# A hybrid decoder layer on one core: a filler 64 bytes smaller, and another order in which a group's PSUM banks are emptied

## The chip, the cores and the metric

The kernel runs on one core of a Trainium2 chip. The metric is the device time of one execution in microseconds. The kernel before took 1816.91 us, the median of three runs (1816.64 to 1817.56 us).

## What is computed

One layer over 272 tokens (16 meta tokens and 256 others) of width 4096: a norm, one input projection to 16384 columns, sixteen heads of stick-breaking attention beside sixteen groups of a short convolution, and an output projection.

```python
h = rmsnorm(x, norm_g)
p = h @ w_in                      # 4096 -> q, k, v, g_attn, b, c, h, z: 8 x 2048
o = stick_breaking_attention(heads(q), heads(k), heads(v))
o = group_rmsnorm(o * silu(g_attn), attn_norm_g, 16)
y = b_conv * short_conv(c_conv * h_conv, conv_w)
y = group_rmsnorm(y * silu(z_conv), conv_norm_g, 16)
return x + concatenate([o, y]) @ w_out
...
return rmsnorm(hs, final_norm_g)[:, N_META:]
```

Everything is float32. The two projections are nearly all of the work.

## The kernel before

**The split.** TensorE multiplies in fp32r. Each weight piece of 128x1024 floats comes by DMA into a ring of five (`raw`). ScalarE casts it to its high part (`wh`, line 408), VectorE subtracts that to get the low part (`wl`, line 404), and each product is three matmuls: low by high, high by high, high by low. Rings of six hold `wh` and `wl`, and the casts run about five pieces ahead of TensorE.

**Pieces.** The program is one list of pieces, and instructions stand in each engine's queue in the order in which the code issues them. The first projection has eight groups `g`, each of two heads with their two convolution groups. Pieces of kind `p` are blocks of k, v, c and h: four pieces per block with the weights stationary and the tokens `xs` moving, 24 matmuls each, summed in a bank called `mm` (lines 441 to 443). Pieces `A`, `B`, `T`, `U` make the four remaining outputs with tokens stationary and weights moving, 512 columns wide (lines 449, 451, 452). For 14 of the 16 pairs of row blocks in a group from 1 on they use seven products in place of eight, for which sums of tokens (`sum`, `lent`) and of weights (`tt`) are made on the way.

**Eight PSUM banks.** Such a group has eight sums, one to a bank: four that are output quarters (D11, D12, D21, D22, the numbers 0 to 3) and four that are products to be shared among the quarters (P1, P5, P7, P6, the numbers 4 to 7). Sum q of group g lies in bank (q + 4g) mod 8, so that the next group's D sums use the banks of this group's P sums, and the other way round. A group has a first zone, in which only its D banks fill, and a second, in which all eight do. D22 is copied out between the two (`open_rows`) and its bank serves the blocks of the second zone.

**The end of a group.** After the last `U` piece of a group, the two last pieces of a block in D22's bank follow. In that time `evict` (lines 650 to 671) empties the seven other banks: ScalarE copies P1, and VectorE adds the products to the quarters, with the results in the tiles `cq` and `cb` (two rows of 512 floats each). What follows on TensorE is the last block of the group (head 1, kind h). Its bank is the one that held D11 (`block_bank`), so its first matmul waits until VectorE has read D11. Transposes of q for the attention (`qT`) and the next group's first pieces come behind that block's first half. Group 0 has no products, and its evict is four ScalarE copies.

**Order.** Nothing is sorted by costs: `later` gives small tasks (softmax, norm, transposes) a piece behind which they are issued, and `evict` is issued one piece after the group's last `U`. The second projection has four groups of the same kind and a thin rest of 256 columns (`mo`, lines 945 to 947); two of its eight weight pieces lie in tiles called `keep`, the others in the rings.

**Memory.** The pools are laid out one behind the other: constants, the small buffers `wk`, the rings `wp`, then the token sums and later the mixed rows `mixh` and `mixl`. The tokens `xs`, and after them the tail's tiles (`res`, `keep`, `osum`), are laid out from the other end. Fillers with the names `pad_...` hold nothing and only move what lies behind them. In the built program `wh0` starts at byte 61120 of a partition, `mixh0` at 114368, `xs0` at 147264 and the first `keep` at 212864.

Of the kernel before, what the change touches and what calls it, by code (L numbers as in the profile page):

```python
# [8 lines left out]
F32 = mybir.dt.float32  # L9
# [3 lines left out]
ALU = mybir.AluOpType  # L13
AX = mybir.AxisListType

P = 128
# [102 lines left out]
def kernel(ctx, tc, xt, xin, xm, par, fg, w1, w2, out):  # L119
# [3 lines left out]
    wk = ctx.enter_context(tc.tile_pool(name="wk", bufs=1))  # L123
    wp = ctx.enter_context(tc.tile_pool(name="wp", bufs=4))

    wp.tile([P, 56], F32, name="pad_w", bufs=1)
    wk.tile([P, 32], F32, name="pad_wk")
    pp = ctx.enter_context(tc.tile_pool(name="pp", bufs=1, space=bass.MemoryType.PSUM))
    dp = ctx.enter_context(tc.tile_pool(name="dp", bufs=1, space=bass.MemoryType.DRAM))

# [303 lines left out]
    psum = {}  # L434
# [22 lines left out]
    D11, D12, D21, D22, P1, P5, P7, P6 = range(8)  # L457
# [85 lines left out]
    V, A, G, T = nc.vector, nc.scalar, nc.gpsimd, nc.tensor  # L543
# [106 lines left out]
    def evict(g):  # L650
        s = gr[g]
        cq = s["cq"] = wk.tile([P, 2, 512], F32, tag="cq", name=f"cq{g}")
        cb = s["cb"]
        if g:
            p1, p5, p7, p6 = (psum.pop((g, q)) for q in (P1, P5, P7, P6))
            A.copy(out=cq[:, 0], in_=p1)
            V.tensor_tensor(out=cb[:, 0], in0=p6, in1=cq[:, 0], op=ALU.add)
            V.tensor_tensor(out=cq[:, 1], in0=p7, in1=cb[:, 0], op=ALU.add)
            V.tensor_tensor(out=cb[:, 1], in0=p5, in1=cb[:, 1], op=ALU.add)
            V.tensor_tensor(out=cb[:, 0], in0=p5, in1=cb[:, 0], op=ALU.subtract)  # L660
            V.tensor_tensor(out=cb[:, 1], in0=cb[:, 1], in1=cq[:, 1], op=ALU.subtract)
        for q, d in ((D11, cq[:, 0]), (D21, cq[:, 1]), (D12, cb[:, 0])):
            if g:
                V.tensor_tensor(out=d, in0=psum.pop((g, q)), in1=d, op=ALU.add)  # L664
            else:
                A.copy(out=d, in_=psum.pop((g, q)))
        if not g:
            A.copy(out=cb[:, 1], in_=psum.pop((g, D22)))
        for c, q in (("cq", "h"), ("cb", "c")):
            v = s[c].rearrange("p t (u w x) -> p t u w x", u=2, w=2)  # L670
            s[q] = v[:, :, :, 0, :], v[:, :, :, 1, :]
# [349 lines left out]
    for i in range(1 - SPLITS, n):  # L1021
# [28 lines left out]
        if i < n1:  # L1050
# [4 lines left out]
            if i in top.values():  # L1055
                later(i + 1, evict, p[1])
                if p[1] == GROUPS - 1:
                    open_mix(0)
            if i == n1 - 1:
                open_tail()  # L1060
        elif p[0] in "ABTUmk":
            g = p[1]
# [96 lines left out]
```

## Time and profile before

The profile is of one execution. Its chain of waits, its groups by line and its timeline are used below.

| | |
|---|---|
| median of three runs | 1816.91 us |
| the profiled execution's own time | 1819.97 us |
| its span, first to last instruction | 1818.2 us |
| VectorE busy | 1561.5 us (86%) |
| ScalarE busy | 1211.2 us (67%) |
| DMA, mean | 221 GB/s |
| first and last matmul | 1.1 us; 1806.6 us |
| granted TensorE clock | 0.998 |

A row of the groups reads: line, engine, operation, the tile written and those read, shape and count; then the busy time in us and the mean of one in ns; then the idle time just before them on that engine and what ended it. In the timeline, a row gives start and length in us, and in brackets the idle time of the engine before it. Matmuls overlap: one of 0.28 us is followed by the next after about 0.12 us, so lengths of matmuls don't add up, and starts do.

### The profile page before, as it was taken

Reading aid. Unit: us, or ns where it says so; the run is one execution under the profiler, and the core shown is the slowest. Engines: PE = TensorE matmul, PEld = TensorE weight load, DVE = VectorE, ACT = ScalarE, POOL = GpSimd, SP = SyncE. Lnnn points to the kernel's source line nnn. Section 1 sums busy time; section 2 is a strip of 40 time slices with the busy share of each in tenths; the row PEclk is TensorE's granted clock in tenths of the full one; section 3 lists DMA queues with packets and bytes.
Section 4 is the critical chain, followed back from the end, with each engine's and each line's share of the span. In section 5 each row is a group of like instructions: output and inputs, shape, how many; then the busy total and the mean of one; then the engine's idle time right before and its main releaser. Section 6 shows DMA issues by size and latency. Waiting matters only on the chain.

```text
span 1818.2 us, 29724 instructions
## 1 busy us (share of the span) xinstructions
PE 1794.0 (99%) x10968; PEld 1622.2 (89%) x10968; DVE 1561.5 (86%) x1936; ACT 1211.2 (67%) x2018; POOL 132.6 (7%) x176
## 2 busy tenths in 40 slices
PE   9999999999999999999999999999999999999997
PEld 7899999899989998899889988999899988888897
DVE  6775889888988898889888988898889898989895
ACT  6755776777667766776677667766776776555563
POOL 2131001010101010101010101010001010000000
PEclk9999999999999999999999999999999999999999
DMA  8877466756675667566756675667566677676665
GB/s 311 311 247 247 160 221 215 249 174 224 216 243 175 229 213 242 177 230 212 241 179 225 215 242 179 225 217 240 178 226 219 227 228 251 208 250 203 197 219 193
DMA packets 118515, 402.57 MB, mean 221 GB/s; under 512 B 13280, under 2 KB 18528, under 8 KB 118368
## 3 DMA queue, kind: packets, MB, share of 16 engines
q1 hardware_dynamic: 114336, 396.99, 65.7%
q10 hardware_dynamic: 4032, 3.67, 0.6%
q8 instruction: 86, 1.41, 0.3%
q14 instruction: 61, 0.50, 0.1%
HBM read 388.03 MB, written 12.58 MB: 220 GB/s over the span
## 4 chain that ended last, share of the span: by engine, by line
PE 88%; DVE 4%; ACT 4%; issue 2%; DMA 2%; ACTq 0%; DVEq 0%; SPq 0%
PE P L449 16%; PE P L451 16%; PE P L452 16%; PE mm L441 12%; PE mm L443 12%; PE mm L442 12%; ACT wh L408 2%; DVE wl L404 2%; DMA raw<-w 1%; ACT vv L577 1%; PE mo L947 0%; PE mo L945 0%; PE mo L946 0%; PE po L812 0%; PE z L756 0%
## 5 line engine op out<-in xcount | busy, mean ns | idle before, releaser
L404 DVE TENSOR_TENSOR wl<-raw,wh 128x1024 fp32r<-128x1024 f32 (+3 forms) x766 | 864.4, 1151 | 157.4 <-ACT wh L408 145.2
L408 ACT CAST wh<-raw 128x1024 fp32r<-128x1024 f32 (+3 forms) x766 | 723.1, 973 | 318.3 <-PE mm L442 88.4
L441 PE MATMUL mm<-xs,wh 128*128 128x258 f32 (+1 forms) x2048 | 589.9, 288 | 8.8 <-DVE cq L664 7.8
L442 PE MATMUL mm<-xs,wh 128*128 128x258 f32 (+1 forms) x2048 | 585.8, 286 | 0.0
L443 PE MATMUL mm<-xs,wl 128*128 128x258 f32 (+1 forms) x2048 | 585.5, 286 | 0.0
L441 PEld LDWEIGHTS mm<-xs,wh 128*128 128x128 f32 x2048 | 385.4, 188 | 15.9 <-ACT wh L408 10.1
L442 PEld LDWEIGHTS mm<-xs,wh 128*128 128x128 f32 x2048 | 385.4, 188 | 3.9
L443 PEld LDWEIGHTS mm<-xs,wl 128*128 128x128 f32 x2048 | 387.1, 189 | 0.0
L408 ACT CAST wh<-t 128x1024 fp32r<-128x1024 f32 (+1 forms) x118 | 123.2, 1044 | 171.3 <-DVE t L425 123.9
L449 PE MATMUL P<-wh,xs 128*128 128x512 f32 x534 | 211.5, 396 | 1.6 <-ACT wh L408 1.6
L451 PE MATMUL P<-wh,xs 128*128 128x512 f32 x534 | 210.4, 394 | 0.0
L452 PE MATMUL P<-wl,xs 128*128 128x512 f32 x534 | 209.1, 392 | 0.0
L449 PE MATMUL P<-wh,mixl 128*128 128x512 f32 (+1 forms) x412 | 155.8, 378 | 0.0
L452 PE MATMUL P<-wl,mixh 128*128 128x512 f32 (+1 forms) x412 | 155.0, 376 | 0.0
L451 PE MATMUL P<-wh,mixh 128*128 128x512 f32 (+1 forms) x412 | 155.0, 376 | 0.0
L404 DVE TENSOR_TENSOR wl<-t,wh 128x1024 fp32r<-128x1024 f32 (+1 forms) x118 | 144.1, 1221 | 6.2 <-ACT wh L408 6.2
L425 DVE TENSOR_TENSOR t<-raw,raw 128x1024 f32<-128x1024 f32 (+1 forms) x118 | 144.0, 1220 | 0.0
L452 PEld LDWEIGHTS P<-wl,xs 128*128 128x128 f32 x534 | 100.6, 188 | 23.1
L449 PEld LDWEIGHTS P<-wh,xs 128*128 128x128 f32 x534 | 100.7, 189 | 19.9 <-ACT wh L408 1.9
L451 PEld LDWEIGHTS P<-wh,xs 128*128 128x128 f32 x534 | 100.9, 189 | 16.8
L449 PE MATMUL P<-wh,lent 128*128 128x512 f32 x252 | 101.1, 401 | 0.0
L451 PE MATMUL P<-wh,lent 128*128 128x512 f32 x252 | 98.7, 392 | 0.0
(247 smaller groups left out, 2086.0 us busy)
## 6 DMA issues: line engine op xcount, KB each, us to landing
raw<-w SPq DMA_DIRECT2D x614, 512.0 KB, 4.4
lent<-sumd SPq DMA_DIRECT2D x63, 512.0 KB, 6.1
raw<-w SPq DMA_DIRECT2D x32, 384.0 KB, 3.8
sumd<-lent SPq DMA_DIRECT2D x9, 512.0 KB, 5.8
raw<-xin SPq DMA_DIRECT2D x8, 512.0 KB, 5.7
raw<-mixd SPq DMA_DIRECT2D x8, 512.0 KB, 4.7
xr<-xt SPq DMA_DIRECT2D x15, 272.0 KB, 5.1
res<-xin SPq DMA_DIRECT2D x12, 256.0 KB, 4.7
```

Of the source, the lines that this page charges most:

```text
L404: nc.vector.tensor_tensor(out=lo[:, c], in0=t[:, c], in1=h[:, c].bitcast(F32), op=ALU.subtract)
L408: nc.scalar.copy(out=h[:, c], in_=t[:, c])
L425: nc.vector.tensor_tensor(out=s[:, :2 * hw].rearrange("p (a b) -> p a b", a=2), in0=a[:, :2 * hw].rearrange("p (a b) -> p a b", a=2), in1= ...
L441: nc.tensor.matmul(out=o, lhsT=h, rhs=x[:, 0, s:], start=k == 0, stop=False)
L442: nc.tensor.matmul(out=o, lhsT=h, rhs=x[:, 1, s:], start=False, stop=False)
L443: nc.tensor.matmul(out=o, lhsT=lo, rhs=x[:, 0, s:], start=False, stop=k == KC - 1)
L449: nc.tensor.matmul(out=o, lhsT=a[1], rhs=h, start=key not in begun, stop=False)
L451: nc.tensor.matmul(out=o, lhsT=a[0], rhs=h, start=False, stop=False)
L452: nc.tensor.matmul(out=o, lhsT=a[0], rhs=lo, start=False, stop=last)
L577: e(out=d[32 * j:32 * j + 32, :, 32 * i:32 * i + 32], in_=s[32 * i:32 * i + 32, :, 32 * j:32 * j + 32])
```

## The change

Two edits.

1. The filler `pad_wk` has 16 floats per partition instead of 32. All tiles of `wk` behind it, the rings, the token sums and the mixed rows start 64 bytes earlier: `wh0` at 61056, `mixh0` at 114304. Tokens, `res`, `keep` and `osum` stay where they are. `wh0` started 64 bytes past a multiple of 128 and now starts at one.
2. In `evict`, for groups 1 to 7, the addition that reads D11 stands second among the eight VectorE additions; it was sixth. The other seven keep their order. For group 0 the four copies stay as they are.

```diff
-    wk.tile([P, 32], F32, name="pad_wk")
+    wk.tile([P, 16], F32, name="pad_wk")
...
+        d11, d21, d12 = (psum.pop((g, q)) for q in (D11, D21, D12))
         if g:
             p1, p5, p7, p6 = (psum.pop((g, q)) for q in (P1, P5, P7, P6))
             A.copy(out=cq[:, 0], in_=p1)
-            V.tensor_tensor(out=cb[:, 0], in0=p6, in1=cq[:, 0], op=ALU.add)
-            V.tensor_tensor(out=cq[:, 1], in0=p7, in1=cb[:, 0], op=ALU.add)
-            V.tensor_tensor(out=cb[:, 1], in0=p5, in1=cb[:, 1], op=ALU.add)
-            V.tensor_tensor(out=cb[:, 0], in0=p5, in1=cb[:, 0], op=ALU.subtract)
-            V.tensor_tensor(out=cb[:, 1], in0=cb[:, 1], in1=cq[:, 1], op=ALU.subtract)
-        for q, d in ((D11, cq[:, 0]), (D21, cq[:, 1]), (D12, cb[:, 0])):
-            if g:
-                V.tensor_tensor(out=d, in0=psum.pop((g, q)), in1=d, op=ALU.add)
-            else:
-                A.copy(out=d, in_=psum.pop((g, q)))
-        if not g:
-            A.copy(out=cb[:, 1], in_=psum.pop((g, D22)))
+            for o, x, y, op in ((cb[:, 0], p6, cq[:, 0], ALU.add), (cq[:, 0], d11, cq[:, 0], ALU.add),
+                                (cq[:, 1], p7, cb[:, 0], ALU.add), (cb[:, 1], p5, cb[:, 1], ALU.add),
+                                (cb[:, 0], p5, cb[:, 0], ALU.subtract), (cb[:, 1], cb[:, 1], cq[:, 1], ALU.subtract),
+                                (cq[:, 1], d21, cq[:, 1], ALU.add), (cb[:, 0], d12, cb[:, 0], ALU.add)):
+                V.tensor_tensor(out=o, in0=x, in1=y, op=op)
+        else:
+            for x, o in ((d11, cq[:, 0]), (d21, cq[:, 1]), (d12, cb[:, 0]), (psum.pop((g, D22)), cb[:, 1])):
+                A.copy(out=o, in_=x)
```

VectorE's queue at the end of group 1, before. The names of the banks' contents are P, the number of the sum and the group, so `P0_1` is D11 and `P7_1` is P6 of group 1; what a row waits for stands behind it.

```order
L404 TENSOR_TENSOR wl163_3889<-raw163_3847,wh163_3888 128x1024 [waits DMAHW1_49,PE_49,Activation_49]
L657 TENSOR_TENSOR cb1_2269<-P7_1_2318,cq1_3921 128x512 [waits PE_49,Activation_49]
L658 TENSOR_TENSOR cq1_3921<-P6_1_2297,cb1_2269 128x512 [waits DVE_49]
L659 TENSOR_TENSOR cb1_2269<-P5_1_2293,cb1_2269 128x512
L660 TENSOR_TENSOR cb1_2269<-P5_1_2293,cb1_2269 128x512 [waits DVE_49]
L661 TENSOR_TENSOR cb1_2269<-cb1_2269,cq1_3921 128x512 [waits DVE_49]
L664 TENSOR_TENSOR cq1_3921<-P0_1_2080,cq1_3921 128x512
L664 TENSOR_TENSOR cq1_3921<-P2_1_2084,cq1_3921 128x512 [waits DVE_49]
L664 TENSOR_TENSOR cb1_2269<-P1_1_2088,cb1_2269 128x512
L404 TENSOR_TENSOR wl164_3919<-raw164_3859,wh164_3918 128x1024 [waits DMAHW2_49]
```

The same place of the changed kernel:

```order
L404 TENSOR_TENSOR wl163_3889<-raw163_3847,wh163_3888 128x1024 [waits DMAHW1_49,PE_49,Activation_49]
L662 TENSOR_TENSOR cb1_2269<-P7_1_2318,cq1_3921 128x512 [waits PE_49,Activation_49]
L662 TENSOR_TENSOR cq1_3921<-P0_1_2080,cq1_3921 128x512 [waits DVE_49]
L662 TENSOR_TENSOR cq1_3921<-P6_1_2297,cb1_2269 128x512
L662 TENSOR_TENSOR cb1_2269<-P5_1_2293,cb1_2269 128x512
L662 TENSOR_TENSOR cb1_2269<-P5_1_2293,cb1_2269 128x512 [waits DVE_49]
L662 TENSOR_TENSOR cb1_2269<-cb1_2269,cq1_3921 128x512 [waits DVE_49]
L662 TENSOR_TENSOR cq1_3921<-P2_1_2084,cq1_3921 128x512 [waits DVE_49]
L662 TENSOR_TENSOR cb1_2269<-P1_1_2088,cb1_2269 128x512
L404 TENSOR_TENSOR wl164_3919<-raw164_3859,wh164_3918 128x1024 [waits DMAHW2_49]
```

Only the row that reads `P0_1` has moved, from sixth to second; the readers of P7, P5 and the fourth addition are one place later each, and the last two rows stand where they stood.

TensorE's queue at the place that waits for it, the same in both kernels: the last rows of the block in D22's bank, and the first of the block in D11's (`mm3_3`).

```order
L442 MATMUL mm3_2_3779<-xs7_140,wh160_3855 128x258
L443 MATMUL mm3_2_3779<-xs7_140,wl160_3856 128x258
L441 MATMUL mm3_3_3966<-xs0_133,wh161_3864 128x258 [waits DVE_49,Activation_49]
L442 MATMUL mm3_3_3966<-xs0_133,wh161_3864 128x258
L443 MATMUL mm3_3_3966<-xs0_133,wl161_3865 128x258
```

The third of these rows waits for a count of VectorE's finished instructions, which is that of the row that reads D11; in the changed kernel the count is reached four additions earlier. No row of TensorE, ScalarE, GpSimd or of a DMA queue changes its place.

## The prediction

> **What bounds the kernel now.** I read the page first: busy times, the chain that ended last, the groups of TensorE.
>
> ```profile
> PE 1794.0 (99%) x10968; PEld 1622.2 (89%) x10968; DVE 1561.5 (86%) x1936; ACT 1211.2 (67%) x2018; POOL 132.6 (7%) x176
> PE 88%; DVE 4%; ACT 4%; issue 2%; DMA 2%; ACTq 0%; DVEq 0%; SPq 0%
> L441 PE MATMUL mm<-xs,wh 128*128 128x258 f32 (+1 forms) x2048 | 589.9, 288 | 8.8 <-DVE cq L664 7.8
> L442 PE MATMUL mm<-xs,wh 128*128 128x258 f32 (+1 forms) x2048 | 585.8, 286 | 0.0
> L443 PE MATMUL mm<-xs,wl 128*128 128x258 f32 (+1 forms) x2048 | 585.5, 286 | 0.0
> L449 PE MATMUL P<-wh,xs 128*128 128x512 f32 x534 | 211.5, 396 | 1.6 <-ACT wh L408 1.6
> L449 PE MATMUL P<-wh,mixl 128*128 128x512 f32 (+1 forms) x412 | 155.8, 378 | 0.0
> L449 PE MATMUL P<-wh,lent 128*128 128x512 f32 x252 | 101.1, 401 | 0.0
> ```
>
> TensorE is busy 99% and carries 88% of the chain. Of its large groups one alone has idle time worth a name: the first matmul of a block, 8.8 us, put down to line 664, which is VectorE's reading of D11, D21 and D12. So the question is what TensorE waits for there, and, for the filler, what a matmul costs. The list of waits, for TensorE:
>
> ```profile
> PE mm L441 <- DVE cq L664: 7.8, 6, 1.4
> PE P L449 <- ACT wh L408: 1.6, 1, 1.6
> PE mm L441 <- ACT wh L408: 1.0, 1, 1.0
> PE po L808 <- DVE kT L584: 0.3, 2, 0.2
> ```
>
> Six waits for line 664 and a seventh, of 1.0 us, on a ScalarE cast. Groups 1 to 7 make seven block starts in D11's bank. Is the odd one of the same kind? The timeline there says so:
>
> ```profile
> 360.47 1.05 ACT L408 CAST wh<-raw 128x1024 fp32r<-128x1024 f32 x1 [1.83 <-PE mm L442]
> 360.73 1.28 DVE L664 TENSOR_TENSOR cq<-P,cq 128x512 f32<-128x512 f32 x2
> 361.56 0.36 PE L441 MATMUL mm<-xs,wh 128*128 128x258 f32 x1 [1.01 <-ACT wh L408]
> ```
>
> The first of the two L664 additions ends at about 360.73 + 0.68 = 361.41, the cast at 361.52. The row of TensorE's queue waits for `wh161`, which was cast pieces earlier; this cast is of a later piece and only ended last. I count it as the seventh wait for D11.
>
> **The order, priced.** One end of a group as an example, group 2, from VectorE's and TensorE's timeline:
>
> ```profile
> 538.85 0.69 DVE L657 TENSOR_TENSOR cb<-P,cq 128x512 f32<-128x512 f32 x1 [0.72 <-ACT cq L656]
> 539.57 0.69 DVE L658 TENSOR_TENSOR cq<-P,cb 128x512 f32<-128x512 f32 x1
> 540.18 0.68 DVE L659 TENSOR_TENSOR cb<-P,cb 128x512 f32<-128x512 f32 x1
> 541.23 0.28 PE L443 MATMUL mm<-xs,wl 128*128 128x258 f32 x1
> 541.98 1.28 DVE L664 TENSOR_TENSOR cq<-P,cq 128x512 f32<-128x512 f32 x2
> 542.80 0.36 PE L441 MATMUL mm<-xs,wh 128*128 128x258 f32 x1 [1.30 <-DVE cq L664]
> 543.77 2.89 DVE L404 TENSOR_TENSOR wl<-raw,wh 128x1024 fp32r<-128x1024 f32 x2
> ```
>
> The last matmul before the wait starts at 541.23 and would be followed at 541.35; the next starts at 542.80. The loss is 542.80 - 541.23 - 0.12 = 1.45 us: the idle 1.30, and the 0.16 by which a matmul's length exceeds the distance to the next. Over seven ends that is 8.8 + 7 x 0.16 = **9.9 us**.
>
> In the new order D11 is read where L658 stood: it starts by 539.57 and is done by 540.26, where before it was done at 542.66. TensorE needs it at 541.35, so 1.1 us of cover are left; the wait goes whole, unless the evict itself begins a microsecond later than now. Whether the second addition starts 0.72 us behind the first, as L658 does, or 0.60, as L659 does behind L658, alters nothing but that cover. The longest wait, 1.4 us in the list, is still below the 2.4 us that four additions give.
>
> What is late next? The other readers move back by one addition (0.6 us), and the last two stay. Before TensorE comes to a bank or a result of theirs it has half a block, 24 matmuls of 0.12, twice: 5.8 us from the wait. Its next dependence is the transpose of q, which needs `cq`:
>
> ```profile
> 548.64 0.60 PE L745 MATMUL qT<-ident,cq 128*128 128x128 f32 x4
> ```
>
> It would come at 547.2, and `cq` is complete at 541.98 + 1.28 = 543.3, in the old order and in the new. The two castings' low parts behind the evict are done at 546.7. So nothing takes the wait's place at once. Later on there is a place with little slack, the attention's product `po`, where 0.3 us of waiting is listed. Its chain:
>
> ```profile
> 400.20 0.24 PE P L452
> 400.44 0.12 issue
> 400.56 0.80 DVE wl L404
> ...
> 410.08 0.49 PE po L808 x2
> ```
>
> This chain sets out from a matmul, which frees a slot of the `wl` ring. It moves forward with TensorE, and the slack stays what it is. I cost the order's other effects at nothing; if po were held by something that doesn't move, it would give back up to 1.4 us in each group.
>
> **The filler, bounded.** It adds and removes no instruction. What could change is the length of those that read the moved tiles. The trace has a comparison: `keep` starts at a multiple of 128 bytes, as the rings will, and the rings now start 64 past one. Same line, same shape:
>
> ```profile
> L408 ACT CAST wh<-raw 128x1024 fp32r<-128x1024 f32 x612 | 630.1, 1052 | 280.4 <-PE mm L442 88.4 <-DVE raw L430 67.8 <-issue 48.3
> L404 DVE TENSOR_TENSOR wl<-raw,wh 128x1024 fp32r<-128x1024 f32 x612 | 748.4, 1249 | 150.1 <-ACT wh L408 140.7 <-PE P L451 0.2 <-PE P L452 0.2
> L945 PE MATMUL mo<-wh,mixl 128*128 128x256 f32 x48 | 13.6, 283 | 0.0
> L945 PE MATMUL mo<-keep,mixl 128*128 128x256 f32 x16 | 4.4, 277 | 0.0
> ```
>
> ```profile
> L408 ACT CAST keep<-raw x2: 1050/1051/1052, 1777.0 to 1778.3; 128x1024 fp32r<-128x1024 f32 x2
> L404 DVE TENSOR_TENSOR keep<-raw,keep x2: 1225/1226/1227, 1778.1 to 1779.4; 128x1024 fp32r<-128x1024 f32 x2
> ```
>
> ScalarE's casts don't differ (1051 and 1052 ns), VectorE's subtractions little (1226 and a mean of 1249, both with time to spare). Matmuls do: 6 ns less where the moving operand is `keep`. By that row, if the place alone made it, the 3 x (534 + 412 + 252) = 3594 wide matmuls whose moving operand is a ring tile would gain 3594 x 6 ns = 22 us, as far as the other engines could follow. Against it, from the same line by shape, with the ring tile moving and the stationary operand at a multiple of 128 (`xs` behind its meta tokens) or 64 past one (`mixh`):
>
> ```profile
> L451 PE MATMUL P<-wh,xs 128*128 128x512 f32 x534 | 210.4, 394 | 0.0
> L451 PE MATMUL P<-wh,mixh 128*128 128x512 f32 x314 | 122.2, 389 | 0.0
> ```
>
> There the multiple of 128 is 5 ns dearer. The 3 x 2048 = 6144 block matmuls have a ring tile as stationary operand, which moves to such a place: 6144 x 5 ns = 31 us lost, at most. Two rows speak, with opposite signs and like sizes, and the trace has no matmul in which both operands lie as they will. I take **0** for the filler, between the ends -22 and +31, since the two prices nearly cancel.
>
> The Trainium skill has a rule here, in "SBUF — State Buffer", section "Door 1: The DMA port swizzle": SBUF has lines of 16 bytes, and only crossings of such lines cost. By it a shift by 64 bytes would change nothing, which is the sum that I take; the 283 and 277 ns above, with starts that are all multiples of 16, say that this isn't the whole account.
>
> **Sum.** 9.9 us off the profiled execution's own 1819.97 gives 1810.1; that one is 3.1 us above the median of the runs, 1816.91, and the same 9.9 off the median gives **1807.0**. About 0.2% (3.6 us) is what a measurement of this kernel can tell from no change.
>
> **Rivals.**
>
> 1. Moving operands gain from their new place and the stationary side doesn't pay. For it: the `keep` row. Against it: only 16 such matmuls for each line, and the `xs` row. Full price 1807 - 22 = 1785; half of it 1796.
> 2. Slower: the block matmuls pay for their stationary operand's place, and the moving side gains nothing. For it: 394 against 389. The price is 6144 times what it costs; from 1.6 ns on (9.9 us / 6144) it eats the gain, from 2.2 ns on the kernel is slower by over 0.2%, at 5 ns it stands at 1838, at half that at 1822. Against it: the two rows are of different stages, which have different work beside them, and `xs` and `mixh` differ in more than that place.
> 3. The wait comes back in part, because the evict starts later. It begins behind a ScalarE copy, which stands behind a cast that waited 0.96 us for a weight piece; should such loads land over 1.1 us later against TensorE, it returns, or else po holds. A fifth to a half of the gain is lost: 1809 to 1812.
> 4. The change doesn't do what it says: the first addition, not the place of D11, is what TensorE waits for. The count in TensorE's queue speaks against it. 1817.
>
> **Chances.** Forecast (waits gone, filler within some 3 us) 0.60, rival 1 0.17, rival 2 0.10, rival 3 0.08, rival 4 0.05. The likeliest gives 1807.0. The range 1789 to 1812 holds the forecast, rival 3 and most of rival 1, about 0.8; rival 2's upper end and the last of rival 1 are left out. Faster by over 0.2%: 0.60 + 0.17 + 0.08 = 0.85, and 0.01 of a mild rival 2. Within 0.2%: rival 4 and 0.03 of rival 2. Slower: the rest of rival 2, 0.06.
>
> **What would show it.** Right: no wait of TensorE's `mm` for the additions of line 662, idle 8.8 us before L441 gone, L408 and L404 as long as now, matmuls of `mm` at 282 to 290 ns and of P at 389 to 394. A lasting wait at the block's start refutes the order; other lengths of `mm` or P matmuls, by 2 ns or more, refute the zero for the filler, and tell by their sign which rival it is. New idle time at `po` or at the casts would be rival 3.

## The result and the profile after

| | before | after |
|---|---|---|
| median | 1817.24 us (four runs, 1816.64 to 1819.52) | 1795.07 us (four runs, 1793.85 to 1795.77) |
| ratio of after to before, 95% interval | | 0.9875 [0.9858, 0.9892] |
| the profiled execution's own time | 1819.97 us | 1793.85 us |
| last matmul's end | 1806.6 us | 1780.5 us |

The change takes 22.2 us off the median, 26.1 us between the two profiled executions. From the page of the kernel after, the busy times, the chain and two of TensorE's groups:

```profile
PE 1773.7 (99%) x10968; PEld 1608.3 (90%) x10968; DVE 1560.1 (87%) x1936; ACT 1207.7 (67%) x2018; POOL 134.5 (8%) x176
PE 93%; DVE 3%; issue 2%; ACT 1%; DMA 0%; POOL 0%; SPq 0%; DVEq 0%; ACTq 0%
L441 PE MATMUL mm<-xs,wh 128*128 128x258 f32 (+1 forms) x2048 | 584.6, 285 | 0.0
L449 PE MATMUL P<-wh,mixl 128*128 128x512 f32 (+1 forms) x412 | 155.8, 378 | 0.0
```

TensorE now carries 93% of the chain in place of 88%. The 8.8 us of idle time before L441 are gone, and L441's mean is 3 ns shorter over 2048 matmuls, which no wait explains. The list of waits of the kernel after, TensorE's rows (us in total, times, longest):

```profile
PE po L805 <- DVE kT L584: 4.0, 7, 0.6
PE P L449 <- ACT wh L408: 1.3, 1, 1.3
```

No block waits for D11 any more. A new row stands first: `po`, 0.3 us before, now 4.0 us in seven waits. Both places in the timeline of the kernel after, first the end of group 2, then `po`:

```profile
531.52 0.69 DVE L662 TENSOR_TENSOR cq<-P,cq 128x512 f32<-128x512 f32 x1
533.04 0.28 PE L443 MATMUL mm<-xs,wl 128*128 128x258 f32 x1
533.16 0.29 PE L441 MATMUL mm<-xs,wh 128*128 128x258 f32 x1
...
400.51 0.28 PE L443 MATMUL mm<-xs,wl 128*128 128x272 f32 x1
400.62 2.36 DVE L404 TENSOR_TENSOR wl<-raw,wh 128x1024 fp32r<-128x1024 f32 x2
402.44 0.39 PE L452 MATMUL P<-wl,xs 128*128 128x512 f32 x1
402.90 0.43 DVE L584 TENSOR_TENSOR kT<-mm,rstd 128x272 f32<-128x272 f32 x1
403.39 0.49 PE L805 MATMUL po<-vv,at 128*128 128x128 f32 x2 [0.56 <-DVE kT L584]
```

D11 is read by 531.52 + 0.69 = 532.21, and the block in its bank starts at 533.16, 0.12 behind the matmul ahead of it: 0.95 us of cover. At the other place the block of keys ends on TensorE at about 400.8. VectorE reads its bank (`kT`) only behind two subtractions of low parts, 402.90 to 403.33; `po` takes that bank next and is ready for it at 402.67.

The rest is in the lengths. From the groups with shapes kept apart, first of the kernel before:

```profile
L442 PE MATMUL mm<-xs,wh 128*128 128x272 f32 x1024 | 296.6, 290 | 0.0
L442 PE MATMUL mm<-xs,wh 128*128 128x258 f32 x1024 | 289.2, 282 | 0.0
```

and of the kernel after:

```profile
L442 PE MATMUL mm<-xs,wh 128*128 128x272 f32 x1024 | 293.7, 287 | 0.0
L442 PE MATMUL mm<-xs,wh 128*128 128x258 f32 x1024 | 288.6, 282 | 0.0
L451 PE MATMUL P<-wh,xs 128*128 128x512 f32 x534 | 208.1, 390 | 0.0
L942 PE MATMUL mo<-wh,mixl 128*128 128x256 f32 x48 | 13.6, 283 | 0.0
L942 PE MATMUL mo<-keep,mixl 128*128 128x256 f32 x16 | 4.5, 283 | 0.0
```

Blocks of 272 columns went from 290 to 287 ns, P with tokens from 394 to 390, and the matmuls on `keep` from 277 to 283, although `keep` has not moved. What counts is the spacing, the time from one start to the next. Each matmul's spacing, summed by kind over the whole trace, for the kinds that changed most; a wait's part is taken out of the matmul ahead of it, and the 57 matmuls ahead of a small task have a row of their own:

| us | before | after | difference |
|---|---|---|---|
| the seven waits for D11 | 9.9 | 0 | -9.9 |
| blocks, 272 columns (3072 matmuls) | 388.9 | 379.0 | -9.9 |
| blocks, 258 columns (3063) | 370.0 | 367.3 | -2.7 |
| P with `xs` (1559) | 360.8 | 355.5 | -5.3 |
| P with `lent`, `sum`, `osum` | 323.0 | 321.7 | -1.3 |
| `mo` | 22.6 | 22.9 | +0.3 |
| matmul ahead of a small task, with `po`'s wait | 14.5 | 17.9 | +3.4 |

The sum is -25.4 of the 26.1 us by which the last matmul ends earlier. So the order gave what it was to give, and the filler, which was forecast at 0, gave more than the order: 15.5 us, the other rows taken together.

### The profile page after: what moved, and what is told of

It is laid out like the page before. It is cut to its first block, busy times and chain, and to the rows that moved or that the text cites. A ratio compares the mean times of both kernels' runs of the same rounds, so it can differ in the third digit from the quotient of the medians.

```text
span 1792.1 us, 29724 instructions
## 1 busy us (share of the span) xinstructions
PE 1773.7 (99%) x10968; PEld 1608.3 (90%) x10968; DVE 1560.1 (87%) x1936; ACT 1207.7 (67%) x2018; POOL 134.5 (8%) x176
## 4 chain that ended last, share of the span: by engine, by line
PE 93%; DVE 3%; issue 2%; ACT 1%; DMA 0%; POOL 0%; SPq 0%; DVEq 0%; ACTq 0%
PE P L449 17%; PE P L452 16%; PE P L451 16%; PE mm L441 13%; PE mm L443 13%; PE mm L442 13%; DVE wl L404 2%; ACT wh L408 1%; DVE t L425 0%; PE mo L944 0%; PE mo L943 0%; PE mo L942 0%; PE po L809 0%; PE z L753 0%; PE po L805 0%
## 5 line engine op out<-in xcount | busy, mean ns | idle before, releaser
L441 PE MATMUL mm<-xs,wh 128*128 128x258 f32 (+1 forms) x2048 | 584.6, 285 | 0.0
L441 PEld LDWEIGHTS mm<-xs,wh 128*128 128x128 f32 x2048 | 385.8, 188 | 5.9 <-ACT mfc L729 2.0
L449 PE MATMUL P<-wh,xs 128*128 128x512 f32 x534 | 209.1, 392 | 1.3 <-ACT wh L408 1.3
L451 PE MATMUL P<-wh,xs 128*128 128x512 f32 x534 | 208.1, 390 | 0.0
L449 PE MATMUL P<-wh,lent 128*128 128x512 f32 x252 | 101.1, 401 | 0.0
L452 PE MATMUL P<-wl,lent 128*128 128x512 f32 x252 | 98.4, 390 | 0.0
```

The source lines that it names most:

```text
L441: nc.tensor.matmul(out=o, lhsT=h, rhs=x[:, 0, s:], start=k == 0, stop=False)
L449: nc.tensor.matmul(out=o, lhsT=a[1], rhs=h, start=key not in begun, stop=False)
L451: nc.tensor.matmul(out=o, lhsT=a[0], rhs=h, start=False, stop=False)
L452: nc.tensor.matmul(out=o, lhsT=a[0], rhs=lo, start=False, stop=last)
```

## Experiments

Three theories for the filler. **Own place**: a tile's start decides how long the matmuls take that read it. **Distance**: the start of the moving operand less that of the stationary one, modulo 256 bytes, decides. **Something else at work**: other engines' traffic meets the matmuls' reads. In the kernel before the starts modulo 256 are 192 for the rings, 64 for `xs` and 192 for the mixed rows; blocks read `xs` as moving operand from its start (272 columns) or 56 bytes on (258 columns), and P reads it as stationary operand 64 bytes on. All diffs are against the kernel after.

**The order alone.**

```diff
-    wk.tile([P, 16], F32, name="pad_wk")
+    wk.tile([P, 32], F32, name="pad_wk")
```

> The new order of the additions alone, the filler as before (32 floats). Two effects add (order 9.9 us, filler the rest): 1807.3 us, no wait of the blocks' first matmul for VectorE, matmuls of mm at 290 (272 wide) and 282 to 286 ns (258 wide) as before, waits of po at 0.3 us in all as before. Rival, the order is worth all of it and the matmuls' lengths are a by-product: 1795 us, with the waits of po at 4.0 us.

Measured: 1809.25 us beside 1816.34 of the kernel before, ratio 0.9957 [0.9941, 0.9974], which is 4.7 to 10.7 us. No wait for D11 is left; in the trace the 9.9 us of waiting are gone, and the kinds of matmuls stay within 1.2 us of where they were (272 columns 388.9, P with `xs` 359.6). `po` does not wait for `kT`. The order is worth what its part of the prediction says.

**The filler alone**: the old order of `evict`, with the small filler.

```diff
-            for o, x, y, op in ((cb[:, 0], p6, cq[:, 0], ALU.add), (cq[:, 0], d11, cq[:, 0], ALU.add),
...
+        for q, d in ((D11, cq[:, 0]), (D21, cq[:, 1]), (D12, cb[:, 0])):
+            if g:
+                V.tensor_tensor(out=d, in0=psum.pop((g, q)), in1=d, op=ALU.add)
```

> The smaller filler alone, the additions in the old order. Two effects add: 1805 us, seven waits for D11 of 1 to 1.5 us as before, matmuls of mm 272 wide at 287 ns in place of 290, of P with xs at 390 in place of 394, waits of po at 4.0 us. Rival, the order is worth all: 1817 us.

Measured: 1804.21 us beside 1816.34, ratio 0.9928 [0.9913, 0.9943], 10 to 16 us. Its waits:

```profile
PE mm L441 <- DVE cq L664: 6.7, 6, 1.6
PE po L808 <- DVE kT L584: 3.9, 7, 0.6
```

The waits for D11 are back, 272 columns take 379.0 us as in the kernel after, and `po` waits 3.9 us. The two parts add up: 0.9957 x 0.9928 = 0.9885, against 0.9875. And `po` waits with the filler, not with the order.

**The tokens moved instead**: the rings at their old place, `xs` 64 bytes higher. The distance between the two is that of the kernel after, while each tile lies elsewhere.

```diff
-    wk.tile([P, 16], F32, name="pad_wk")
+    wk.tile([P, 32], F32, name="pad_wk")
...
-    xp.tile([P, 40], F32, name="pad_x")
+    xp.tile([P, 24], F32, name="pad_x")
```

> New order, rings where they were before (64 bytes past a multiple of 128), but the tokens xs moved 64 bytes up by their own filler (24 floats in place of 40). The distance from xs to the rings, modulo 256, is then that of the changed kernel, while each lies elsewhere. If the distance between stationary and moving operand sets a matmul's length: 1795 us, mm 272 wide 287 ns, P with xs 390 ns. If a ring tile's own place does: 1807 us, 290 and 394 ns.

**Both moved**: the rings at the new place and `xs` 64 bytes lower, with the old distance.

```diff
-    xp.tile([P, 40], F32, name="pad_x")
+    xp.tile([P, 56], F32, name="pad_x")
```

> New order, smaller filler, and xs moved 64 bytes down too (its filler 56 floats in place of 40). The distance from xs to the rings is that of before, while the rings lie at multiples of 128 as in the changed kernel. If the distance sets a matmul's length: 1807 us, mm 272 wide 290 ns, P with xs 394 ns. If a ring tile's own place does: 1795 us, 287 and 390 ns.

Measured: with the tokens moved 1795.79 us, ratio 0.9884 [0.9870, 0.9899]; with both moved 1808.67, ratio 0.9955 [0.9941, 0.9970], beside 1816.34. The first equals the kernel after, the second the order alone. Groups by shape, tokens moved:

```profile
L441 PE MATMUL mm<-xs,wh 128*128 128x272 f32 x1024 | 293.5, 287 | 0.0
L451 PE MATMUL P<-wh,xs 128*128 128x512 f32 x534 | 208.5, 390 | 0.0
L942 PE MATMUL mo<-keep,mixl 128*128 128x256 f32 x16 | 4.4, 277 | 0.0
```

and both moved:

```profile
L441 PE MATMUL mm<-xs,wh 128*128 128x272 f32 x1024 | 296.7, 290 | 0.0
L451 PE MATMUL P<-wh,xs 128*128 128x512 f32 x534 | 209.9, 393 | 0.0
L942 PE MATMUL mo<-keep,mixl 128*128 128x256 f32 x16 | 4.5, 282 | 0.0
```

Own place falls: the rings lie at the old place in the first and are fast, at the new one in the second and are slow. `keep` fits too: it never moved, and it has 277 ns where it lies 192 past `mixl` and 282 or 283 where the distance is 0.

**Can another distance do better?** The `keep` row says that 192 is shorter than 0. The sums and mixed rows, stationary under 2,652 P matmuls, lie at distance 0 from the rings; 64 bytes of filler before them make it 192.

```diff
+    sp.tile([P, 16], F32, name="pad_s")
...
+        if g0 == 0:
+            mixp.tile([P, 16], F32, name="pad_m")
```

> The kernel after the change, with the sums, lent tiles and mix tiles of the Strassen products 64 bytes higher, the wh ring where the change put it, so that the moving ring lies 192 bytes (mod 256) past the stationary tiles, as keep did past mix in the kernel before (272 cycles where distance 0 gave 288). Distance theory: the P matmuls with a sum, a lent tile or a mix as stationary operand fall from 391 ns to about 384, mo<-wh from 283 to 277; some 2,400 matmuls by 6.7 ns are up to 16 us, less what the waits for po, kT and the casts take back: 1779 to 1790 us. Rival, own place of a tile (or a length that follows only the moving side): nothing changes, 1795 within 2. Second rival: VectorE is the next bound, the matmul rows shrink as said and waits of TensorE for sums take most of it back: 1788 to 1794 with new waits of P for a DVE or ACT row.

Two more places of `xs` (`pad_x` of 24 and of 72 floats in place of 40):

> The kernel after the change with the filler of the token tiles 64 bytes smaller, so that the tokens xs and the wh ring start at the same place mod 256 (distance 0 both ways). Distance theory: the matmuls that stream 272 tokens over a wh piece go to distance 0, the worst distance seen (+32 cycles): from 287 ns back to about 290, +10 us; the P matmuls with xs stationary go from distance 0 (they count the ring against the xs chunk) by 64 to distance 192: from 391 to about 385, -10 us; sum 1790 to 1800. Rival, own place of the tokens: both groups move the same way, 1785 or 1805.

> The kernel after the change with the filler of the token tiles 128 bytes larger, so that the tokens start 192 bytes lower than in the run beside it. It fills in the map of distances: distance theory says that each group's length depends on the distance alone, so that with a distance of 64 for the streaming of 272 tokens and of 128 for the P matmuls with xs stationary the rows move between 280 and 290 ns and between 384 and 397 ns, independent of each other; no time is forecast beyond 1785 to 1812. Rival, own place of the tokens: the two groups move together and by the same share.

Measured, beside 1816.89 us of the kernel before: sums moved 1809.01, ratio 0.9958 [0.9944, 0.9972]; `xs` on the ring's place 1810.03, 0.9965 [0.9951, 0.9978]; `xs` 64 past it 1811.08, 0.9971 [0.9959, 0.9983]. Going by the ratios, all three are 15 to 17 us slower than the kernel after. For the P matmuls of the first two my own expectation had the sign wrong; the third had its time and its rows within the wide bounds that were given. Groups by shape of the kernel with the sums moved:

```profile
L454 PE MATMUL P<-wh,mixh 128*128 128x512 f32 x314 | 124.2, 396 | 0.0
L454 PE MATMUL P<-wh,lent 128*128 128x512 f32 x252 | 99.6, 395 | 0.0
L444 PE MATMUL mm<-xs,wh 128*128 128x272 f32 x1024 | 293.4, 287 | 0.0
```

The rows with a sum as stationary operand went up by 5 to 6 ns (390 in the kernel after), and the blocks of 272 columns, whose distance stayed, moved by 0.4 us in all. So the distance decides here too, but with 512 columns 0 is the short one and 192 a long one: a row of 256 columns does not speak for 512. With `xs` on the ring's place the blocks of 272 columns take 384.9 us in the table's terms (379.0 after) and P with `xs` 364.6 (355.5); 64 past it 388.9 and 365.1.

Two things in these traces don't follow from a matmul's own distance. Matmuls on `xs` and on sums stand between each other, three by three, and where one kind became longer the other did too, with its distance unchanged: P with `xs` takes 359.5 us in place of 355.5 with the sums moved, and P with `lent`, `sum` and `osum` 325.6 in place of 321.7 with `xs` on the ring's place. And with the sums moved, all `mo` matmuls (256 columns) lie at distance 192, `keep` against `mixl` at the very starts of the kernel before; they take 117.8 ns from start to start, where `keep` took 113.3 there.

**The disputed cost by itself.** Chains of 48 matmuls on data that lies still, nothing else of the kernel. Their stationary tiles `sA` to `sH` and moving tiles `mA` to `mD` lie at chosen places. This program and the next ran once each.

```diff
+    for w in (512, 272, 258, 256):
+        for c in "ABCDEFGH":
+            for k in ops(w, "A", c):
+                nc.tensor.matmul(**k)
...
+    nc.vector.tensor_copy(out=va[:, :256], in_=banks[n[0] % 8][:, :256])
...
+    for i in range(90):
+        nc.vector.tensor_tensor(out=vc, in0=va, in1=vb, op=ALU.add)
```

> Not the kernel's work: chains of 48 matmuls on data that lies still, stationary tiles sA to sH each 32 bytes (mod 256) past the one before, moving tiles mA to mD each 64 bytes past the one before, mA and sA at the same place; first with the other engines idle, each pair of one width; then the stationary tile alternating between sA and another; then the same distances at other places; then four of the distances again while VectorE, ScalarE and the DMA queues work. Distance theory, from the rows of the seven kernels so far: with 512 columns mA with sA is the shortest (start to start 227 ns) and a stationary tile 64, 128 or 192 bytes further on makes it 230 to 233; with 272 columns sC (moving 192 past stationary) is the shortest at 123 ns, sA 125, sE and sG 126.5; pairs of equal distance at other places agree within 1 ns. Rival, the lengths come from the other engines' traffic and not from the pair: all pairs are equal within 0.5 ns in the idle part and differ only in the busy part. Second rival, the load of the next stationary tile is what meets the moving stream: in the alternating chains the matmuls on sA before a load of the other tile are the long ones.

Stretches of this kernel, each with only the matmuls that read one stationary tile: the stretch's bounds and its length, TensorE's busy time, the count, granted clock, share of the DMA engines, GB/s. In this order: `sC`, `sE`, `sG` with `mA` (distances 192, 128 and 64) and 512 columns, then 272 columns in the same order, then `sE` with `mC` (distance 0), 512 and 272 columns:

```profile
34.00:46.00 12.00, 11.36 (x48) 1.00 0.00 0
56.70:68.30 11.60, 11.32 (x48) 1.00 0.01 1
79.00:90.60 11.60, 11.16 (x48) 1.00 0.01 1
113.00:119.60 6.60, 6.09 (x48) 1.00 0.00 0
125.00:131.70 6.70, 6.24 (x48) 1.00 0.01 2
137.00:143.80 6.80, 6.24 (x48) 1.00 0.01 2
303.00:314.30 11.30, 11.08 (x48) 1.00 0.00 0
364.00:370.60 6.60, 6.18 (x48) 1.00 0.00 0
```

A busy time is 47 spacings and one length (0.39 or 0.29 us): with 512 columns (11.36 - 0.39) / 47 = 233 ns at distance 192, 233 at 128, 229 at 64 and 227 at 0; with 272 columns 123 at 192, 127 at 128 and 64, 125 at 0. Read from the starts themselves, in ns, without the first four matmuls of a chain, beside what the starts in the kernels above give where they have that distance (to some 0.3 ns, by how much of a piece's edges is left out):

| columns | distance | chain | kernels |
|---|---|---|---|
| 512 | 0 / 64 / 128 / 192 | 227.3 / 228.9 / 232.4 / 233.4 | 226.8 / 229.0 / 232.5 / 233.2 |
| 272 | 0 / 64 / 128 / 192 | 125.3 / 126.6 / 126.7 / 123.3 | 125.1 / 126.6 / 126.5 / 123.3 |
| 258 | 56 / 120 / 184 / 248 | 120.0 / 117.7 / 120.0 / 119.0 | 119.4 / 118.5 / 120.2 / 119.1 |
| 256 | 0 / 192 | 120.0 / 113.3 | 120.0 / 113.3 (before), 117.8 (sums moved) |

Pairs of the same distance at other places agree within 0.2 ns (512 columns at distance 0: 227.2 to 227.4 at three places), and the last part, with DMA at 0.91 of the engines' time and VectorE and ScalarE busy throughout, gives 226.7, 228.9, 232.3 and 233.4 for 512 columns. So at 512 and 272 columns it isn't traffic. Only 256 columns at 192 differ, 117.8 ns in place of 113.3; traffic doesn't explain that either, since `keep` has 113.3 in the kernel before, where the other engines work too. The alternating chains (`sA` and another tile in turn) do not tell whether the own stationary tile or the next one's load counts. With `sC`, at 512 columns, 228.6 behind `sA` and 231.4 behind `sC` lie on the side of the own tile, but at 272 columns both are near 127.4, longer than either alone. With `sE` at 272 columns, 126.4 behind `sA` and 124.7 behind `sE` are near what the next tile has alone (126.7 and 125.3). That stays open.

**Finer steps**, the moving start shifted by single elements. The numbers in the brackets are starts in elements of 4 bytes.

```diff
+    (512, (0, 0, 1, 2, 3, 4, 8, 12, 20, 28, 36, 44, 52, 60, 61, 62, 63)),
+    (272, (36, 40, 42, 44, 46, 47, 48, 49, 50, 52, 56)),
```

> Not the kernel's work: chains of 48 matmuls on data that lies still, one stationary place, the moving operand's start shifted in steps of 4 to 32 bytes; widths 512, 272, 258, 256, 384, 260 and 264. If the length goes by lines of 64 or 32 bytes, starts between two places of the coarse chains have one of their two lengths; if it goes by the element, lengths change from one start to the next. It shows whether a place exists that is shorter than 544 cycles for 512 columns, or than 296 and 285 for the pair of 272 and 258 (the second starts 56 bytes past the first). No place shorter than these would mean that the kernel after already has the best of them.

Measured, in ns from start to start: with 512 columns 226.7 at 0, 236.6, 233.3, 228.9 and 231.7 at 4, 8, 12 and 16 bytes, 231.1 to 234.7 further on, and 226.7 at 252. With 272 columns 126.6, 123.3, 123.4 and 126.8 at 184, 188, 192 and 196 bytes, and 123.4 at 160 too. Four bytes alter the length, so no line of 16, 32 or 64 bytes is its measure. No place of those tried is shorter than 226.7 for 512 columns or than 123.3 for 272; 258 columns have 117.7 at 120, but with 272 columns 56 bytes before it (126.6 at 64) the pair is dearer than at 192 and 248. The kernel after lies at the best of these places for its blocks and for P with `xs`.

**The new wait at `po`.** First, `po` and the transposes behind it one piece later:

```diff
-        later(t[2], po, g, 0)
-        later(after(t[2], 1), trans, g, 1)
+        later(after(t[2], 1), po, g, 0)
+        later(after(t[2], 2), trans, g, 1)
```

> The kernel after the change with the output projection's first part and the second group's transposes placed one piece later in the order of TensorE's work, so that the bank which po takes has one more piece of time in which VectorE reads the keys' D22 bank. Theory: the seven waits of po for that read (4.0 us in the profile after) go, 1791 to 1792 us. Rival: the piece that is let past ends in the same wait, or the next block's start now waits for po's own bank; 1795 within 1.5, with the 4 us under another name. Second rival: later transposes make the attention part start later, 1797 to 1800.

Measured: 1817.50 us beside 1816.89, ratio 0.9996 [0.9987, 1.0006]; everything gained is gone. Its list of waits:

```profile
PE mm L441 <- DVE cq L813: 19.1, 7, 2.8
```

The rival's place was right and its price far too small. L813 is VectorE's reading of `po`'s bank, which the next block takes; it now comes behind a piece's worth of VectorE's other rows. The timeline there shows a second cost:

```profile
413.41 0.40 PE L452 MATMUL P<-wl,lent 128*128 128x512 f32 x1
416.53 0.36 PE L441 MATMUL mm<-xs,wh 128*128 128x272 f32 x1 [2.72 <-DVE cq L813]
416.73 0.29 PE L442 MATMUL mm<-xs,wh 128*128 128x272 f32 x1
...
418.13 0.43 PE L441 MATMUL mm<-xs,wh 128*128 128x272 f32 x1
418.35 0.43 PE L442 MATMUL mm<-xs,wh 128*128 128x272 f32 x1
418.58 0.43 PE L443 MATMUL mm<-xs,wl 128*128 128x272 f32 x1
```

From 417.2 to 420.4 the starts are 0.227 us apart in place of 0.123, and the profile has a granted clock of 0.50 in that stretch.

Second, VectorE's reading of the keys one row sooner:

```diff
-                later(i + 1, plain_block, *p[1], i)
+                later(i + (p[1][1] > 0), plain_block, *p[1], i)
```

> The kernel after the change with VectorE's reading of each k block (kT) one row of low parts earlier in its queue; nothing else moves. Theory: in the profile after, po waits seven times 0.6 us for that row, which stands behind two subtractions of 1.2 us; one of them let past, it waits no more: about 4 us less, 1790 to 1792. Rival: VectorE is held by the block's last matmul and the low parts come late at the P matmuls, as much as po gains: 1794 to 1796. Second rival: the rotation of buffers shifts and something else waits, as with po one piece later: 1797 or more.

Measured: 1792.43 us (1791.60 to 1794.35) beside 1816.62, ratio 0.9872 [0.9856, 0.9889]. Its waits:

```profile
PE P L449 <- ACT wh L408: 1.4, 1, 1.4
PE po L805 <- DVE vt L590: 1.3, 7, 0.2
```

`po` waits 1.3 us in place of 4.0, and the last matmul ends 2.2 us earlier (1778.3 against 1780.5), but the intervals of the two ratios overlap almost wholly. It is the fastest kernel run here; that it beats the kernel after is not shown by these times.

## Why the prediction was right and wrong

- **What bounds the kernel: right.** TensorE, with the waits for D11 as its only idle time of size, and the odd seventh wait, listed under a cast, was one of them: all seven went together, with the order alone.
- **The order at 9.9 us: right.** The trace's 9.9 us went to 0; the order alone measured 7.1 us between medians, with an interval of 4.7 to 10.7 that holds the term. The cover was forecast at 1.1 us and is 0.95.
- **"The slack stays what it is" at `po`: wrong, a small term.** It holds while only the waits go (no wait of `po` for `kT` with the order alone), as the chain was read. With shorter matmuls TensorE comes to `po` sooner, and VectorE, which has no idle time over 0.1 us between 395.02 and 403.25 in the trace after, does not: +3.4 us. The filler alone brings it too, 3.9 us of waiting with the old order. What the prediction held against itself came true: a `po` held by something that doesn't move gives time back, 0.5 us a group in place of the 1.4 that it allowed at most.
- **The filler at 0: the step that failed.** It was worth 10 to 16 us alone, and so the forecast of 9.9 us became 22.2. The prediction's own sign against the zero, lengths that differ by 2 ns or more, came: 287 ns for 290 in the blocks of 272 columns, 390 for 394 in P with `xs`. The two rows that set its bounds (`keep` against `wh`, `xs` against `mixh`) were read as prices of a tile's own place, one for each operand, which nearly cancelled. Both rows show the distance of two tiles: `keep` 192 past `mixl` against `wh` at 0, and `wh` 64 past `xs` against 0 past `mixh`. Read so, with the tiles' starts, the second row gives the gain of P with `xs` straight away: its distance becomes 0, that of `mixh`. The blocks' distance of 192 at 272 columns stood in no row of before, so it could not be priced from that trace; the middle of two misread prices had nothing behind it. That 1795.07 lies within the range of 1789 to 1812 is owed to the share that rival 1 had in it, not to the forecast.
- **Rivals.** The first, moving operands gain from their place, has the sign but not the mechanism: the largest gain, the blocks' 9.9 us, came where the ring is the stationary operand, and `keep` became longer. Half its price, 1796, lies beside the measured time by luck: it stood for 11 us in the wide P matmuls, which gave some 7. The second had the blocks pay for the ring's place; they gained. The third was right in where a wait would come back, `po`, but for another reason than a late evict. The fourth is refuted by the order alone.
- **The rule of the Trainium skill** ("SBUF — State Buffer", section "Door 1: The DMA port swizzle"), by which an access that crosses to a new line of 16 bytes pays a penalty, was read as the only cost of a place, and so as no change for a shift by 64 bytes. The runs disagree with that reading: 64 bytes made 10 to 16 us, and at 272 columns the distances 192 and 208, which lie alike in such lines, take 123.4 and 126.5 ns.

## What to carry to other kernels

Where TensorE is busy nearly throughout, look at the starts of matmuls of one shape with different operands: a few ns between them, at thousands of matmuls, can be worth more than the waits, here 15.5 us against 9.9. Note the byte addresses of both operands and compare by their difference, in the same width alone, before a filler is priced; a chain of 48 matmuls on still data foretold the kernels' spacings to 0.5 ns at 272 and 512 columns and to 0.8 at 258, but at 256 columns and distance 192 it missed one kernel by 4.5. And a gain on the bounding engine is to be held against each engine that doesn't speed up with it: `po`, which had waited 0.3 us in all, came to wait 4.0.

## What the hardware showed

- **Length by distance.** In these chains a matmul in fp32r of 256 columns takes 113.3 to 120.0 ns from start to start, one of 512 columns 226.7 to 236.6, by the difference of its operands' starts modulo 256 bytes, down to steps of 4 bytes, and at 272 and 512 columns the same idle or with the other engines at work. At 256 columns and 192 something else counts as well: 113.3 ns in the idle chain and for `keep` in the kernel before, 117.8 in the busy chain and in the kernel with the sums moved. Why that is, and why the best distance differs by width (0 at 512, 188 to 192 at 272, 192 at 256), is not known from these runs. The Trainium skill ("TensorE: Matmul & The Clock Gate", section "Back-to-back issue gap") has a formula for the gap by width alone, 216 ns at 512 columns; every chain here is above it, and the formula has no term for the place.
- **A short wait can halve the clock.** In the kernel with `po` later, TensorE idles seven times for 2.7 us. Behind five of them the granted clock is 0.5, for 3.4 us and once for 6.8, and 13 to 27 matmuls start 0.227 us apart in place of 0.123; behind the waits of 1.3 us in the kernel before, none do. That took another 9.2 us (272 columns 388.2 in place of 379.0), half as much as the waits themselves. The Trainium skill (the same page, section "HAM oscillation — how this bites in real kernels") has the clock fall with idle gaps of over some 3.4 us; here 2.7 us were enough, in five cases of seven. The traces show what sets the five apart: the granted clock changes only on a fixed grid of 3.41 us, and in the five cases 2.1 to 2.7 us of the wait lie within one cell of it, in the other two at most 1.7. In the traces of all eleven kernels, a cell at clock 1 with up to 1.8 us of idle time was followed by one at 1, and every cell with 1.9 us or more by one at 0.5.
